# Order of work at the head of an FFN stage, and one ScalarE copy in a block product

## The chip, the cores and the metric

The kernel runs on one core of a Trainium2 chip. The metric is the time of one execution in microseconds on the device, as the median of several runs. Five engines work side by side, each through its own queue in program order: TensorE (matmuls, out of SBUF into PSUM), VectorE, ScalarE, GpSimd (POOL in the profile) and SyncE (SP, which issues most of the loads).

## The reference

A trunk of two layers over 512 tokens of width 1024, in fp32. Each layer is a gated FFN, a token mixer and a second gated FFN; each of the three takes a normalised input that is scaled and shifted by a vector from the condition c (adaLN).

```python
c_act = jax.nn.silu(c)
for l in range(DEPTH):                      # DEPTH = 2
    mod = c_act @ ada_w[l] + ada_b[l]       # nine vectors of 1024
    ...
    f = swiglu(modulate(rmsnorm(h, ln_ffn1[l]), sh1, sc1), ffn1_wg[l], ffn1_wu[l], ffn1_wd[l])
    h = h + MACARON_WEIGHT * gt1[:, None, :] * f
    ...                                     # the mixer, then the second FFN in the same form
# swiglu(x, wg, wu, wd) = (silu(x @ wg) * (x @ wu)) @ wd, inner width 2816
```

## The kernel before

**Layout and precision.** The activations are held transposed, 128 features by 512 tokens a tile. Each fp32 matmul is done as three faster ones: both operands are split into a rounded high half and a low half (`wh`, `wl` for a weight, `uh`, `ul` for the normalised input, `ah`, `al` for the FFN's inner columns), and high by high, high by low and low by high are added up in PSUM. ScalarE makes a high half with a copy, VectorE the low half with a subtraction (`halves`, L300; `split`, L888).

**Stages.** The program is FFN, mixer, FFN, for two layers: four FFN stages, which begin near 0, 1060, 1430 and 2425 us, and two mixers. The weights come as units of 128 output columns, in a fixed list. `w_split` (L317) splits the next unit or part of a unit; `w_ahead(lead)` (L353) goes on splitting until `lead` quarters of a unit lie ready; `w_get` (L357) takes a unit and then splits ahead by `4 * ahead` quarters, 7 in an FFN stage. `w_fill` (L349) keeps 3 or 4 units of raw weights ordered from SP.

**FFN inner columns.** There are 22 of them, each with a gate and an up product. The first four (six in the first stage) are plain products: `dense`, 24 matmuls of 512 tokens. Of these the first two columns (four in the first stage) are multiplied already at the end of the stage before, in `tail` (L629) or `start` (L782), and handed on as PSUM banks `pss`. The other columns go in pairs through `dense_pair` (L389): a 2 by 2 block product in seven parts instead of eight, each 12 matmuls of 256 tokens, in three banks mX, mZ and mY. The parts use sums and differences of blocks of the weights (`ws`, made by POOL and by accumulating loads) and of the input (`th`, `tl`, made by `halves_sums`, L590: half by POOL, half by VectorE). The parts go X, Z, X, Y, X, Z, X; after each, ScalarE copies the bank into `c`, or VectorE adds the bank to `c`, and a part that accumulates further in the same bank has to wait for that. Down products follow after two or three pairs, in four chunks.

**What sets the order.** Each engine works through its instructions in the order in which the program emits them. Work that runs beside the products lies in lanes of generators (`run`, `step`, L174): every third (in a pair every sixth) matmul makes a `tick`, and at a tick each generator in the lane `post` goes one step, if an estimated clock that the program keeps says that its inputs are there. The sums of the input, the gates and the products of a pair run in that lane; `drain("post")` before the first pair (L935) and before each down chunk (L946) emits what is left of it. At each tick `ada_tick` (L470) also adds `rate` to a counter, and at 1 a step of adaLN is emitted: one load of 256 KB four steps ahead, and one VectorE operation with c. What is not done by the first down chunk is done there at one go (`ada_need`, L478).

**Head of a stage.** At the end of `tail`, after the halves of the input are made, `w_ahead(4)` (L775; 12 ahead of the mixer) splits one unit, `halves_sums` is put in the lane, and the last products of the first columns are emitted. Then `ffn` (L895) loads c anew and computes its silu (`c_load`, L156; `c_silu`, L162: a tanh on ScalarE and one VectorE operation for each half of c), and finishes the first columns one after the other: tanh on ScalarE, `g` and `ay` on VectorE, `ah` on ScalarE, `al` on VectorE. Nearly all tiles come from one pool of 84 buffers (`NBIG`); a load or an operation that takes a buffer waits until its last reader is done.

Of the kernel before, what the change touches and what calls it, by code (L numbers as in the profile page):

```python
# [58 lines left out]
def trunk(ctx: ExitStack, tc: tile.TileContext, x, c, ada_w, ada_b, ln, w_gu, w_dn, w_in, w_ba, conv_w,  # L59
# [17 lines left out]
    def big(s, shape=(128, 512), dt=F32):  # L77
        return bigp.tile(list(shape), dt, name=nm(s), tag="big")
# [77 lines left out]
    def c_load():  # L156
        for i in range(2):
            caT[i] = big("ca")
            nc.sync.dma_start(out=caT[i], in_=bass.AP(tensor=c.tensor, offset=c.offset + 512 * i,
                                                      ap=[[0, 128], [1, 512]]))  # L160

    def c_silu():  # L162

        for i in range(2):
            t = big("ct")
            A.activation(out=t, in_=caT[i], func=AF.Tanh, scale=0.5)
            V.scalar_tensor_tensor(out=caT[i], in0=t, scalar=1.0, in1=caT[i], op0=OP.add, op1=OP.mult)
# [185 lines left out]
    def w_ahead(lead):  # L353
        while st["split"] < len(jobs) and st["lead"] < lead:
            w_split()
# [26 lines left out]
    def dense(key, xs):  # L382
        w = w_get(key)
        ps = bank("mm")
        lst = passes(w, xs, range(len(xs)))
        mm_list([(ps, a, b, i == 0, i == len(lst) - 1) for i, (a, b) in enumerate(lst)])
        return ps

    def dense_pair(keys, us, ts):  # L389

        X, Y, Z = bank("mX"), bank("mY"), bank("mZ")
        c1, c2 = big("c1"), big("c2")
        lo, hi = HALF

        def b(k0, sl):
            return [(us[k][0][:, sl], us[k][1][:, sl]) for k in range(k0, k0 + 4)]

        def copy(out, ps):  # L400
            A.activation(out=out, in_=ps[:, lo], func=AF.Copy)

        def add(out, ps):
            V.tensor_tensor(out=out, in0=ps[:, lo], in1=out, op=OP.add)

        for j, (ps, x, first, fn, out) in enumerate((
                (X, b(0, lo), True, copy, c1[:, lo]), (Z, ts[0], True, copy, c2[:, hi]),
                (X, ts[1], False, copy, c1[:, hi]), (Y, b(4, lo), True, add, c1[:, lo]),
                (X, ts[2], False, add, c2[:, hi]), (Z, b(4, hi), False, add, c1[:, hi]),
                (X, ts[3], False, copy, c2[:, lo]))):  # L410
            w = w_get(keys[0], part=j)
            lst = passes(w, x, range(4), lo)
            mm_list([(ps[:, lo], a_, b_, first and i == 0, i == len(lst) - 1)
                     for i, (a_, b_) in enumerate(lst)], 2 * Q)
            fn(out, ps)
        return c1, c2
# [212 lines left out]
    def tail(keys, xs, gt, nxt, Gs, adds):  # L629
# [142 lines left out]
            low = nlow  # L772
            mm_list(lt[8 + 3 * k:11 + 3 * k])
        low()
        w_ahead(12 if any(narrow) else 4)  # L775
        ts = None if any(narrow) else halves_sums(yt)
        for k in range(NF):
            first(k, 1)
# [3 lines left out]
    def start(l, keys):  # L782
# [99 lines left out]
        for g in (64, 96):  # L882
            V.tensor_tensor(out=sel, in0=sel, in1=ident[:, g:g + 16], op=OP.add)
        w_fill()
        w_ahead(4)
        return us, pss, halves_sums(ys)

    def split(y, s):  # L888
# [6 lines left out]
    def ffn(l, f, us, pss, ts, nxt):  # L895
        act = {}
        st.update(ahead=AHEAD, raw=4)
        ada.update(rate=0.13, stop=min(len(ada_seq), 144 * l + 96 * f + 80))
        if (l, f) != (0, 0):
            c_load()  # L900
            c_silu()
        seq = ffn_order(first_gu(l, f))

        def gate(cs, done):

            for c_, sign in zip(cs, (0.5, -0.5)):
                t = big("t")
                A.activation(out=t, in_=c_, func=AF.Tanh, scale=sign)
                yield
                V.scalar_tensor_tensor(out=c_, in0=t, scalar=1.0, in1=c_, op0=OP.add, op1=OP.mult)  # L910
                done.append(c_)
                yield

        def product(i, gs, done, ups):
            for j, (c_, y) in enumerate(zip(gs, ups)):
                while len(done) <= j:
                    yield False
                V.tensor_tensor(out=y, in0=c_, in1=y, op=OP.mult)
                yield
                act[i + j] = split(y, "a")  # L920
                yield
        gt = None
        for kind, i in seq:
            if kind == "gu":
                pg, pu = (pss.pop(0) if pss else dense(("gu", l, f, i, q), us) for q in range(2))
                t = big("t")
                A.activation(out=t, in_=pg, func=AF.Tanh, scale=0.5)
                g2 = big("g2")
                V.scalar_tensor_tensor(out=g2, in0=t, scalar=1.0, in1=pg, op0=OP.add, op1=OP.mult)
                y = big("ay")  # L930
                V.tensor_tensor(out=y, in0=g2, in1=pu, op=OP.mult)
                act[i] = split(y, "a")
            elif kind == "pair":
                if i == first_gu(l, f):
                    drain("post")  # L935
                g2s = dense_pair([("pair", l, f, j, 0) for j in (i, i + 1)], us, ts)
                done = []
                run("post", gate(g2s, done))
                ups = dense_pair([("pair", l, f, j, 1) for j in (i, i + 1)], us, ts)
                run("post", product(i, g2s, done, ups))  # L940
            else:
                if gt is None:
                    g_ = ada_need(l, 6 * f + 2)
                    gt = small("gt", [128, NF])
                    V.tensor_scalar(out=gt, in0=g_, scalar1=0.25, scalar2=None, op0=OP.mult)
                drain("post")  # L946
                lo, hi = CHUNKS[i]
                xs = [act.pop(j) for j in range(lo, hi)]
                last = i == len(CHUNKS) - 1
                st["ahead"] = 4 if last else AHEAD  # L950
                if last:
                    ada["rate"] = 0.0
                    Gs = gains(*nxt[:2]) if nxt else (None, None)
                    adds = []
                o = 0
                while o < (NF - TAIL if last else NF):
                    if last and o:
                        st["ahead"] = 3 + o
                    if last and o == 0:
                        pd = dense_late([("dn", l, f, i, q) for q in range(3)], xs)  # L960
                    else:
                        pd = [dense(("dn", l, f, i, o), xs)]
                    for p in pd:
                        V.scalar_tensor_tensor(out=h[o], in0=p, scalar=gt[:, o:o + 1], in1=h[o],
                                               op0=OP.mult, op1=OP.add)
                        if last:
                            norm_acc(o, adds)
                        o += 1
        return tail([("dn", l, f, i, q) for q in range(NF - TAIL, NF)], xs, gt, nxt, Gs, adds)


# [632 lines left out]
```

## Time and profile before

| | us |
|---|---|
| median of three runs | 2786.26 |
| the three runs | 2776.88, 2786.26, 2789.63 |
| the profiled execution | 2783.32 |
| its span, from the first to the last instruction | 2781.5 |

| engine | busy us | share of the span |
|---|---|---|
| TensorE | 2687.2 | 97% |
| VectorE | 2014.8 | 72% |
| ScalarE | 1262.1 | 45% |
| GpSimd | 867.1 | 31% |

The times of rows are counted from the first instruction. PE is TensorE, DVE VectorE, ACT ScalarE, POOL GpSimd. A row names the tile that is written, an arrow and the tiles that are read. What stands in square brackets or behind the last bar is the idle time of the engine before it, and which instruction ended it.

### The profile page before, as it was taken

Reading aid. Unit: us, or ns where it says so; the run is one execution under the profiler, and the core shown is the slowest. Engines: PE = TensorE matmul, PEld = TensorE weight load, DVE = VectorE, ACT = ScalarE, POOL = GpSimd, SP = SyncE. Lnnn points to the kernel's source line nnn. Section 1 sums busy time; section 2 is a strip of 40 time slices with the busy share of each in tenths; the row PEclk is TensorE's granted clock in tenths of the full one; section 3 lists DMA queues with packets and bytes.
Section 4 is the critical chain, followed back from the end, with each engine's and each line's share of the span. In section 5 each row is a group of like instructions: output and inputs, shape, how many; then the busy total and the mean of one; then the engine's idle time right before and its main releaser. Section 6 shows DMA issues by size and latency. Waiting matters only on the chain.

```text
span 2781.5 us, 48295 instructions
## 1 busy us (share of the span) xinstructions
PE 2687.2 (97%) x17332; PEld 2372.4 (85%) x17332; DVE 2014.8 (72%) x3889; ACT 1262.1 (45%) x2594; POOL 867.1 (31%) x1285
## 2 busy tenths in 40 slices
PE   6899999999999998999989999999999999989998
PEld 4789998888878888899988989888888888989997
DVE  8787878676655678787788877776665566787676
ACT  5344445555533334454444544445554333354443
POOL 4232304453450005123142322254445200224231
PEclk9999999999999999999999999999999999999999
DMA  7476732342344545766536776323323546256552
GB/s 275 132 221 183 180 109 95 107 120 74 109 137 152 172 143 153 206 189 179 166 102 196 192 189 164 130 68 111 103 75 101 152 163 220 90 167 175 144 147 65
DMA packets 254529, 407.12 MB, mean 146 GB/s; under 512 B 52816, under 2 KB 69968, under 8 KB 254288
## 3 DMA queue, kind: packets, MB, share of 16 engines
q1 hardware_dynamic: 231568, 358.93, 40.6%
q0 software_dynamic: 22720, 45.10, 9.2%
q8 instruction: 136, 2.23, 0.3%
q14 instruction: 105, 0.86, 0.1%
HBM read 382.95 MB, written 11.53 MB: 142 GB/s over the span
## 4 chain that ended last, share of the span: by engine, by line
PE 85%; DVE 8%; ACT 2%; issue 2%; DMA 2%; POOL 0%; SPq 0%; DVEq 0%; ACTq 0%
PE mm L122 50%; PE mX L122 13%; PE mZ L122 6%; PE tl L122 4%; PE mY L122 3%; DVE wl L122 3%; PE as L122 1%; DVE c L122 1%; PE ob L122 1%; DVE ad L122 1%; PE pw L122 1%; PE pq L122 1%; PE aT L122 1%; PE po L122 1%; DVE tl L122 1%
## 5 line engine op out<-in xcount | busy, mean ns | idle before, releaser
L122 DVE TENSOR_TENSOR wl<-wr,wh 128x512 fp32r<-128x512 f32 (+1 forms) x936 | 676.7, 757 | 180.0 <-ACT wh L122 175.1
L122 ACT ACTIVATE wh<-wr 128x512 fp32r<-128x512 f32 (+1 forms) x936 | 517.1, 595 | 143.7 <-PE mm L122 110.8
L122 PE MATMUL mm<-uh,wh 128*128 128x512 f32 (+1 forms) x1488 | 411.9, 385 | 36.7 <-ACT wh L122 24.7
L122 PE MATMUL mm<-uh,wl 128*128 128x512 f32 (+1 forms) x1488 | 406.7, 378 | 0.0
L122 PE MATMUL mm<-ul,wh 128*128 128x512 f32 (+1 forms) x1488 | 357.1, 374 | 1.6 <-DVE ul L122 1.6
L122 PEld LDWEIGHTS mm<-uh,wh 128*128 128x128 f32 x1488 | 276.7, 193 | 87.5 <-ACT wh L122 27.2
L122 PEld LDWEIGHTS mm<-uh,wl 128*128 128x128 f32 x1488 | 278.9, 191 | 44.4 <-issue 0.7
L122 PEld LDWEIGHTS mm<-ul,wh 128*128 128x128 f32 x1488 | 256.6, 189 | 44.3 <-DVE ul L122 2.3
L122 ACT ACTIVATE c<-mX 128x256 f32<-128x256 f32 x210 | 80.5, 383 | 367.0 <-PE mX L122 366.4
L293 POOL DMA_DIRECT2D wr<-in_w_gu_dram x70 | 61.6, 880 | 512.3 <-DVE wl L122 189.4
L122 DVE SCALAR_TENSOR_TENSOR ad<-ad,ca 128x512 f32<-128x512 f32 x272 | 193.6, 726 | 0.4 <-PE mm L122 0.2
L122 POOL TENSOR_SCALAR y<-y,G,mod 128x256 f32<-128x256 f32 (+1 forms) x88 | 64.7, 737 | 350.5 <-DVE y L122 200.8
L122 POOL TENSOR_TENSOR ws<-wr,wr 128x512 f32<-128x512 f32 x70 | 97.4, 1392 | 225.2 <-DMA wr<-in_w_gu_dram 40.5
L122 DVE TENSOR_TENSOR wl<-ws,wh 128x512 fp32r<-128x512 f32 x210 | 161.4, 775 | 7.8 <-ACT wh L122 6.1
L122 PE MATMUL mm<-ah,wh 128*128 128x512 f32 x608 | 159.7, 391 | 1.3 <-ACT wh L122 1.0
L122 PE MATMUL mm<-ah,wl 128*128 128x512 f32 x608 | 158.2, 389 | 0.0
L122 PE MATMUL mX<-th,wh 128*128 128x256 f32 x840 | 138.7, 288 | 20.0 <-DVE c L122 17.8
L122 PE MATMUL mm<-al,wh 128*128 128x512 f32 x608 | 158.0, 389 | 0.0
L122 DVE SCALAR_TENSOR_TENSOR h<-mm,gt,h 128x512 f32<-128x512 f32 x120 | 88.9, 748 | 80.9 <-PE mm L122 80.6
L122 PEld LDWEIGHTS mX<-th,wh 128*128 128x128 f32 x840 | 115.9, 192 | 25.2 <-DVE c L122 21.6
L122 PE MATMUL mX<-tl,wh 128*128 128x256 f32 x840 | 135.8, 284 | 0.0
L122 PE MATMUL mX<-th,wl 128*128 128x256 f32 x840 | 135.6, 284 | 0.0
(318 smaller groups left out, 5400.5 us busy)
## 6 DMA issues: line engine op xcount, KB each, us to landing
wr<-in_w_gu_dram SPq DMA_DIRECT2D x352, 256.0 KB, 4.3
ad<-in_ada_w_dram SPq DMA_DIRECT2D x288, 256.0 KB, 4.2
wr<-in_w_in_dram SPq DMA_DIRECT2D x264, 256.0 KB, 3.2
wr<-in_w_dn_dram SPq DMA_DIRECT2D x128, 256.0 KB, 3.2
ws<-in_w_gu_dram SPq DMA_DIRECT2D x70, 256.0 KB, 4.3
wr<-in_w_gu_dram POOLq DMA_DIRECT2D x70, 256.0 KB, 4.3
ws<-in_w_gu_dram POOLq DMA_DIRECT2D x70, 256.0 KB, 6.5
wr<-in_w_dn_dram SPq DMA_DIRECT2D x96, 128.0 KB, 3.1
```

The lines of the kernel that those rows point to most:

```text
L122: return fn(*args, **kw)
L293: nc.gpsimd.dma_start(out=out, in_=src, accum_op=OP.add)
```

## The change

The change has four parts. (1) In `tail` and in `start`, `w_ahead(12)` splits three units at the head of each stage instead of one (ahead of the mixer it was 12 already). (2) In `ffn` the columns that are handed on as banks are finished stage by stage: all tanh, then all `g` and `ay`, then all splits. (3) In the three later FFN stages c is still loaded at once, but its silu is computed by a generator after 24 ticks, and adaLN steps start only then. (4) In the fifth of the seven parts of `dense_pair`, ScalarE copies the bank mX to a new tile `c3`, and VectorE adds `c3` to `c` instead of adding the bank.

```diff
         c1, c2 = big("c1"), big("c2")
+        c3 = big("c3")[:, :256]
...
+        def copy_add(out, ps):
+            copy(c3, ps)
+            V.tensor_tensor(out=out, in0=c3, in1=out, op=OP.add)
...
-                (X, ts[2], False, add, c2[:, hi]), (Z, b(4, hi), False, add, c1[:, hi]),
+                (X, ts[2], False, copy_add, c2[:, hi]), (Z, b(4, hi), False, add, c1[:, hi]),
...
-        w_ahead(12 if any(narrow) else 4)
+        w_ahead(12)
...
         w_fill()
-        w_ahead(4)
+        w_ahead(12)
         return us, pss, halves_sums(ys)
...
         if (l, f) != (0, 0):
+            ada["rate"] = 0.0
             c_load()
-            c_silu()
+
+            def late():
+                for _ in range(24):
+                    yield False
+                c_silu()
+                ada["rate"] = 0.13
+
+            run("post", late())
...
         gt = None
-        for kind, i in seq:
+        there = [(pss[2 * i], pss[2 * i + 1]) for i in range(len(pss) // 2)]
+        tanhs, ys = [big("t") for _ in there], [big("ay") for _ in there]
+        for (pg, _), t in zip(there, tanhs):
+            A.activation(out=t, in_=pg, func=AF.Tanh, scale=0.5)
+        for (pg, pu), t, y in zip(there, tanhs, ys):
+            V.scalar_tensor_tensor(out=t, in0=t, scalar=1.0, in1=pg, op0=OP.add, op1=OP.mult)
+            V.tensor_tensor(out=y, in0=t, in1=pu, op=OP.mult)
+        for i, y in enumerate(ys):
+            act[i] = split(y, "a")
+        for kind, i in seq[len(there):]:
             if kind == "gu":
-                pg, pu = (pss.pop(0) if pss else dense(("gu", l, f, i, q), us) for q in range(2))
+                pg, pu = (dense(("gu", l, f, i, q), us) for q in range(2))
```

## Rows read from the trace of the kernel before

**Rows 1.** The page's first part: busy time, share of the span, instructions.

```profile
PE 2687.2 (97%) x17332; PEld 2372.4 (85%) x17332; DVE 2014.8 (72%) x3889; ACT 1262.1 (45%) x2594; POOL 867.1 (31%) x1285
```

**Rows 2.** TensorE's waits: who for whom; us in total, times, longest.

```profile
PE mm L122 <- ACT wh L122: 25.8, 6, 6.7
PE mX L122 <- DVE c L122: 17.8, 19, 2.2
...
PE mZ L122 <- ACT th L122: 7.9, 1, 7.9
...
PE mX L122 <- ACT c L122: 2.2, 3, 1.0
```

**Rows 3.** Busy time by stretch: length, each engine (instructions), granted clock, DMA share, GB/s.

```profile
90.60:95.12 4.52, 4.52 (x11) 3.55 (x12) 4.45 (x11) 3.55 (x7) 1.57 (x2) 0.50 0.64 104
118.97:122.43 3.46, 3.46 (x16) 3.46 (x17) 2.70 (x5) 2.68 (x6) 0.00 (x0) 0.50 0.15 24
193.80:197.50 3.70, 3.70 (x19) 3.70 (x19) 1.55 (x4) 0.90 (x2) 1.78 (x2) 0.54 0.44 86
1070.10:1076.79 6.69, 0.00 (x2) 0.00 (x1) 5.01 (x8) 2.49 (x6) 0.00 (x0) 0.85 0.62 196
1076.79:1081.57 4.78, 4.78 (x11) 3.84 (x12) 4.78 (x6) 4.07 (x8) 4.24 (x4) 0.50 0.15 55
...
2442.30:2446.90 4.60, 4.60 (x11) 3.63 (x12) 4.60 (x6) 4.07 (x8) 4.05 (x4) 0.50 0.16 57
...
1099.00:1139.00 40.00, 38.33 (x314) 37.88 (x315) 32.85 (x63) 20.63 (x46) 5.89 (x5) 1.00 0.64 189
```

**Rows 4.** Timeline of TensorE, head of the second FFN stage: start, us, instructions.

```profile
1068.13 1.98 PE L122 MATMUL mm<-ul,wh 128*128 128x512 f32 x8
1076.79 3.78 PE L122 MATMUL mm<-uh,wh 128*128 128x512 f32 x8 [6.69 <-ACT wh L122]
```

**Rows 5.** Timeline of ScalarE, the same head.

```profile
1072.81 0.63 ACT L122 ACTIVATE ah<-ay 128x512 fp32r<-128x512 f32 x1 [2.54 <-DVE ay L122]
...
1076.12 2.17 ACT L122 ACTIVATE wh<-wr 128x512 fp32r<-128x512 f32 x4
```

**Rows 6.** Timeline of VectorE, the same head.

```profile
1057.66 1.29 DVE L122 TENSOR_TENSOR wl<-wr,wh 128x512 fp32r<-128x512 f32 x2
...
1070.02 1.28 DVE L122 SCALAR_TENSOR_TENSOR ca<-ct,ca 128x512 f32<-128x512 f32 x2
...
1073.47 0.69 DVE L122 TENSOR_TENSOR al<-ay,ah 128x512 fp32r<-128x512 f32 x1 [0.78 <-ACT ah L122]
...
1076.86 4.11 DVE L122 TENSOR_TENSOR wl<-wr,wh 128x512 fp32r<-128x512 f32 x4
```

**Rows 7.** Timelines of TensorE and VectorE, head of the first FFN stage.

```profile
90.60 3.78 PE L122 MATMUL mm<-uh,wh 128*128 128x512 f32 x8 [4.70 <-ACT wh L122]
...
79.42 0.69 DVE L122 SCALAR_TENSOR_TENSOR g<-t,mm 128x512 f32<-128x512 f32 x1 [8.47 <-ACT t L122]
...
90.67 2.49 DVE L122 TENSOR_TENSOR wl<-wr,wh 128x512 fp32r<-128x512 f32 x4
```

**Rows 8.** Timelines of VectorE and ScalarE in a later pair of columns.

```profile
1285.88 1.77 DVE L122 SCALAR_TENSOR_TENSOR c<-t,c 128x512 f32<-128x512 f32 x1
...
1290.71 0.38 ACT L122 ACTIVATE c<-mX 128x256 f32<-128x256 f32 x1 [5.12 <-PE mX L122]
```

**Rows 9.** Groups of instructions: count, busy us, mean ns, idle before, what ended it.

```profile
L122 ACT ACTIVATE wh<-wr 128x512 fp32r<-128x512 f32 (+1 forms) x936 | 517.1, 595 | 143.7 <-PE mm L122 110.8 <-DVE wl L122 26.0 <-DMA wr<-in_w_gu_dram 3.7
...
L122 DVE SCALAR_TENSOR_TENSOR ad<-ad,ca 128x512 f32<-128x512 f32 x272 | 193.6, 726 | 0.4 <-PE mm L122 0.2
...
L122 ACT ACTIVATE c<-mX 128x256 f32<-128x256 f32 x210 | 80.5, 383 | 367.0 <-PE mX L122 366.4
...
L122 DVE TENSOR_TENSOR c<-mX,c 128x256 f32<-128x256 f32 x70 | 29.4, 420 | 4.2 <-PE mX L122 3.6
```

**Rows 10.** The page's part on loads: count, KB each, median us to landing.

```profile
ad<-in_ada_w_dram SPq DMA_DIRECT2D x288, 256.0 KB, 4.2
```

## The prediction

> **What bounds the kernel now.** I read the share of each engine first: TensorE is busy for 97% of the span [rows 1], so a change can only win what TensorE waits, and what it loses in clock after a wait. The second view is TensorE's waits by releaser [rows 2]: 25.8 us in six waits for a rounded weight (wh) from ScalarE, 17.8 us in nineteen waits of a product's bank mX for VectorE's add into c, 7.9 us in one wait for a rounded sum (th). The third view is the granted clock by stretch [rows 3]. In the 6.69 us without a matmul at 1070 the clock falls, and the next 4.78 us run at 0.50, the lower level of 1.2 GHz, so half of them, 2.4 us, is lost on top. At 193.80, after one of the longest waits on mX (2.2 us [rows 2]), it is near 0.5 for 3.4 of 3.7 us: 1.7 us lost.
>
> So there are three sums to win. **Heads of the three later FFN stages** (1070, 1439, 2436 us): the 25.8 us less 4.7 us in the first stage [rows 7] and about 1 us elsewhere leave 20 us; with half of 4.8, 4.3 (taken between its neighbours) and 4.6 us at the lower clock [rows 3], 27 us. **First stage**: 4.7 us [rows 7] and 7.9 us [rows 2], with half of 4.52 and of 3.46 us [rows 3]: 16.5 us. **Bank mX**: 17.8 us [rows 2] and twice 1.7 us [rows 3] (a second such stretch follows one more of the longest waits): 21 us. Together 64 us of an execution of 2783.3 us.
>
> Why TensorE waits at a head: ScalarE rounds the four halves that it needs at 1076.12 [rows 5], in program order behind the two splits ah, and those wait for VectorE's ay. VectorE is in one unbroken queue from the last low half of u on: two wl for the one unit that is split early (1057.66), the sums until 1070.02, c's silu (2 in 1.28 us), then the two finished columns with a stop of 0.78 us before an al, since ah of the same column is only then on its way [rows 6]. The weights stand behind all of it.
>
> **Part 1, three units split ahead (tail and start).** The units for the next dense products are split before the sums are queued. This moves four wh (0.54 us each, from 2.17 us for four [rows 5]) and four wl forward. Alone, four wl take 2.49 us [rows 7]; beside POOL (busy for 4.24 of the 4.78 us there [rows 3]) 4.11 us [rows 6]. They now stand right behind the two wl that went at their plain 1.29 us [rows 6], so I take 2.5 us; the upper bound is 4.1. They delay the sums by that, and TensorE needs no sum until the first pair. TensorE's program is unchanged: 8 matmuls of 512 columns take about 1.8 us [rows 4], less their overlap, a unit 5.5. Its second, third and fourth unit now go 1070.1, 1075.6, 1081.0, and the first pair begins at 1086.5; now it is 1076.79 and three units and the 2.4 us of slow clock, 1095.7: 9 us later. The fourth unit is split after the two finished columns; VectorE's queue to there is six wl (3.7 us), the sums (11 us from 1058.9 to 1070.0 [rows 6]) and two columns without stops (4.2): about 1077, and two wl more make 1078, for need at 1081 to 1083. The loads are no issue: the raw weights are ordered earlier, and ScalarE's wh waited for a weight load for 3.7 us in the whole run [rows 9].
>
> **Part 2, first columns stage by stage.** Both tanh go first, then both g and y, then the splits. The adds and multiplies are the same; the stops of 0.78 us before al [rows 6] go, 1.5 us of VectorE at a later head and 3 us in the first stage, where there are four columns. Banks come free no later. Cost nothing, since ScalarE is idle there (2.54 us before one ah [rows 5]).
>
> **Part 3, c later.** The silu of c (1.28 us of VectorE at 1070.02 [rows 6]) moves behind 24 ticks, three dense products. With it the first adaLN step moves from the first to the fourth unit, and its four loads are only ordered then. Two prices. A load takes 4.2 us to land [rows 10], behind up to five other loads on SP's queue; VectorE reaches the step at about 1088 (1078, a column 2.9, seven wl 4.4, the last low sums 1.2, c's silu 1.3), and behind it in its queue stand the product of the fourth unit and the weights of the pair's second half, needed at 1096.6. A late landing costs TensorE between 0 and about 4 us a head; I take 0.5, since seven parts (10 us of TensorE) are split by then. Second, three steps fewer are done by the first down product, where the rest is done in one go: 3 times 0.73 us [rows 9] more in VectorE's queue, 2.2 us, of which 0 to 2.2 reach TensorE; no wait of its own stood there before, so I take 0.3.
>
> A later head then gives 9 less 0.5, less 0.5 for the tighter queue at the pair, so 8; three give 24 us, a last subtraction for the down product leaves 23. **First stage:** VectorE idles 8.47 us before the first g [rows 7]; the four wl move into that hole and save 2.5 us, the stops 3 us. TensorE's 4.7 us disappear, but it then stands longer for th, which is released by VectorE's whole queue: the gain is the queue's, 5.5 to 6.5 us, not 16. I take 6; the bounds are 3 (POOL's second sum sets the end) and 10.
>
> **Part 4, the closest half product copied by ScalarE.** Of the seven parts, the fifth and the seventh both use mX, with only the sixth (12 matmuls of half the width, about 1.4 us) between. VectorE's add of the fifth is 0.42 us [rows 9], but stands in its queue behind operations that POOL stretches: at 1285.88 one of 1.77 us [rows 8], with a wait of TensorE behind it. ScalarE then stands idle for 5.12 us, until its next copy at 1290.71 [rows 8]. A copy of this shape takes 0.38 us there [rows 9], 70 of them 27 us off the path. What ScalarE's copies out of mX already cost shows in the same view: 2.2 us in three waits, out of 140 such hand-overs [rows 2]; one more in 70 pairs costs about 1.1 us. So 21 less 1: 20 us. The lower bound is 0, if VectorE's lateness stops TensorE at the weights instead; VectorE is busy 32.85 of 40 us with two pairs [rows 3], and the seven parts of lead are 10 us against a lateness of 2, so I take 20.
>
> Against this stands a rule. The add had one operand in PSUM and keeps at 420 ns in the mean over 70 [rows 9]; its new form reads two SBUF operands, as wl does, whose four took 2.49 us in one place and 4.11 us beside POOL's adds [rows 6, 7]. The Trainium skill (SBUF — State Buffer, "Who interferes with whom") says that VectorE and GpSimd share one pair of SBUF ports under a lock, and that a VectorE operation with two SBUF inputs falls under it. The trace agrees. By that rule each add could wait for a GpSimd operation. By rows alone the price is at most 1.77 less 0.6 us [rows 8], 1.2 us of VectorE in a pair of 20 us, and it is off TensorE's path so long as VectorE has its 18% of slack; it is counted in the second rival.
>
> **Sum.** 23 + 6 + 20 = 49 us off the profiled execution of 2783.3 us: 2734. That execution lies 3 us below the median of the runs shown, so 2737 us. With all of 27, 10 and 21 it would be about 2728; with the weak ends of the parts (15, 3, 13) 2755: own range 2724 to 2757, with the spread of runs.
>
> **Rivals.** *The head's wait only changes its releaser* (to th, or to the parts of the first pair). For it: the first stage, where 7.9 us stand for th right after the weights were there, behind a VectorE queue that is as full at the later heads. Against: there the second sums are queued early, ahead of the finished columns. The heads would give 5 instead of 23: 2755. Chance 0.14.
>
> *VectorE is the bound in the pairs.* Waits on mX go, and come back as waits for wl. For it: 82% busy with POOL's stretches, and the port lock. Against: its lateness of 2 us against a lead of 10. mX gives 2 instead of 20: 2755. Chance 0.13.
>
> *Buffers, slower.* The later products, tanh tiles and four more split tiles hold some 8 of the pool's 84 buffers longer, and c3 one in each pair; loads on SP wait for buffers. If loads go late enough, wh waits for data. Each of 70 pairs would pay what its load is late beyond its lead; it decides when a weight lands more than about 10 us later than now. At 1.5 us a pair it is 105 us, less the 49: 2843. Against: the 3.7 us of such waits [rows 9], which say that loads have room. Chance 0.06.
>
> *The reordering does little*: the order in which the sums are queued follows an estimated clock, which the earlier splits shift, so that gains at the heads and mX are mostly given back in the same stage. About 2776. Chance 0.09.
>
> **How the numbers follow.** Forecast 0.58 at 2737. The first two rivals are faster too. A difference under 0.5% (14 us) is about what cannot be told from none here. Faster: 0.58 + 0.14 + 0.13 = 0.85, less 0.01 for their tails: 0.84; same 0.09; slower 0.07. The range goes from 2722, all parts full and a fast median, to 2765, which takes in both faster rivals; it leaves out the last two.
>
> **What would show it.** Right: no wait of several us for wh at the later heads and no lower clock there; mX waits for ScalarE in a few waits of under 1 us; at the first stage one wait, for th, longer than 7.9 us but ending some 6 us earlier. Wrong: mZ or mX at the first pair of a head waiting for th or wl, a VectorE stop before the first adaLN step released by its load, or mm waiting at the first down product. The forecast falls if such new waits add up to over 20 us.

## The result and the profile after

| | before | after |
|---|---|---|
| median, us | 2785.11 (4 runs, 2776.88 to 2789.63) | 2742.46 (4 runs, 2740.16 to 2743.25) |
| ratio, 95% interval | | 0.9849 [0.9825, 0.9873] |
| profiled execution | 2783.32 | 2742.23 |
| its span | 2781.5 | 2740.4 |

The change saves 43 us, 1.5%. The page of the kernel after begins with the span and the busy times:

```profile
span 2740.4 us, 48441 instructions
...
PE 2677.2 (98%) x17332; PEld 2369.2 (86%) x17332; DVE 2005.9 (73%) x3889; ACT 1286.4 (47%) x2664; POOL 867.1 (32%) x1285
```

TensorE does the same 17332 matmuls. Its busy time is 10.0 us shorter than in [rows 1], with a mean granted clock of 0.993 instead of 0.990; the other 31.1 of the 41.1 us of span are idle time of TensorE that is gone. Which waits went is told by its waits (who for whom; us in total, times, longest):

```profile
PE mX L122 <- ACT c L122: 14.0, 5, 5.2
...
PE mZ L122 <- ACT th L122: 5.5, 2, 4.6
...
PE mm L122 <- ACT wh L122: 1.6, 4, 0.8
```

Against [rows 2], the 17.8 us for VectorE's add into c are gone altogether, 25.8 us for a weight have become 1.6, and 7.9 us for th have become 5.5. One line is new in size: mX for ScalarE's copy into c, 2.2 us before, is now 14.0 us. Three of its five waits, 12.8 us, stand at the three later heads, and the clock falls behind each. Three stretches by window, each from such a wait's end on (length, then busy time of PE, PEld, DVE, ACT, POOL with instructions, granted clock, DMA share, GB/s):

```profile
1080.23:1084.30 4.07, 4.07 (x19) 4.07 (x20) 2.72 (x7) 2.36 (x6) 0.00 (x0) 0.50 0.65 209
...
1436.70:1442.70 6.00, 6.00 (x28) 6.00 (x29) 4.06 (x9) 2.68 (x6) 0.00 (x0) 0.50 0.67 218
...
2424.18:2429.20 5.02, 5.02 (x23) 5.02 (x24) 4.58 (x7) 2.68 (x6) 1.53 (x1) 0.50 0.54 160
```

So the lower clock of [rows 3] is not gone from the heads; it has moved a few microseconds on.

Since both kernels issue their matmuls in one and the same order, the n-th matmul can be looked up in both timelines, and the difference of its two starts tells what has been won up to there. Read at the borders of the stages:

| part of the execution | won, us | forecast, us |
|---|---|---|
| start and head of the first stage | 0.1 + 8.2 | 6 |
| heads of the second, third and fourth stage | 2.9 + 3.6 + 3.6 = 10.1 | 23 |
| pairs and what follows, four stages | 6.7 + 8.3 + 5.5 + 3.3 = 23.8 | 20 |
| first mixer | -0.8 | 0 |
| sum | 41.4 | 49 |

The heads gave less than half of what was forecast. Here is the second head, on TensorE, ScalarE and VectorE (timelines: start, us, instruction; in brackets the idle time before and what ended it):

```profile
1072.04 0.64 PE L122 MATMUL mX<-uh,wh 128*128 128x256 f32 x4
...
1074.43 0.64 PE L122 MATMUL mZ<-tl,wh 128*128 128x256 f32 x4
1080.23 1.22 PE L122 MATMUL mX<-th,wh 128*128 128x256 f32 x4 [5.16 <-ACT c L122]
```

```profile
1075.12 0.57 ACT L122 ACTIVATE t<-mm 128x512 f32<-128x512 f32 x1
1078.76 0.63 ACT L122 ACTIVATE ah<-ay 128x512 fp32r<-128x512 f32 x1 [3.07 <-DVE ay L122]
1079.30 0.61 ACT L122 ACTIVATE wh<-wr 128x512 fp32r<-128x512 f32 x1
1079.82 0.36 ACT L122 ACTIVATE c<-mX 128x256 f32<-128x256 f32 x1
```

```profile
1071.17 1.29 DVE L122 TENSOR_TENSOR wl<-wr,wh 128x512 fp32r<-128x512 f32 x2
...
1075.38 1.28 DVE L122 SCALAR_TENSOR_TENSOR ca<-ct,ca 128x512 f32<-128x512 f32 x2
1076.59 0.68 DVE L122 SCALAR_TENSOR_TENSOR ad<-ad,ca 128x512 f32<-128x512 f32 x1
...
1077.98 0.69 DVE L122 TENSOR_TENSOR ay<-g,mm 128x512 f32<-128x512 f32 x1
```

The pair begins at 1072.04. Its first part fills bank mX by about 1073.6, and its third part goes into the same bank. ScalarE's copy that empties the bank stands in ScalarE's queue behind ah of the fourth column, the last one ahead of the pairs. That ah waits for VectorE's ay, and ay is the end of a VectorE queue without a gap from 1070.56 on: a low half al, the low halves of the pair's first weights, c's silu, an adaLN step, g, ay. ScalarE idles for 3.07 us with the copy behind it, and TensorE for 5.16.

The same chain was there before. These are the same steps in the kernel before, on TensorE and on ScalarE:

```profile
1095.47 0.64 PE L122 MATMUL mX<-uh,wh 128*128 128x256 f32 x4
...
1099.15 0.75 PE L122 MATMUL mX<-th,wh 128*128 128x256 f32 x4 [0.65 <-ACT c L122]
```

```profile
1097.68 0.63 ACT L122 ACTIVATE ah<-ay 128x512 fp32r<-128x512 f32 x1 [5.02 <-DVE ay L122]
1098.21 0.61 ACT L122 ACTIVATE wh<-wr 128x512 fp32r<-128x512 f32 x1
1098.73 0.36 ACT L122 ACTIVATE c<-mX 128x256 f32<-128x256 f32 x1
```

The copy was already late, by 0.65 us. All three waits of the line mX for ScalarE in [rows 2] stand at this place of the three later heads: 0.65, 1.03 and 0.57 us. The whole program stands 14.2 us earlier at this head. From 1095.47 to 1072.04 are 23.4 us, so the pair begins 9.2 us earlier on top of that; ah goes from 1097.68 to 1078.76, 18.9 us, only 4.7 on top. And 0.65 + 9.2 - 4.7 = 5.2 us, the wait that is measured. TensorE was moved ahead by 9, VectorE's queue by 4.7, and a head can win no more than the queue does; of these 4.7 the lower clock takes half of 4.07 us back.

### The profile page after: what moved, and what is told of

The parts are those of the page before. It is cut to its first block, busy times and chain, and to the rows that moved or that the text cites. A ratio compares the mean times of both kernels' runs of the same rounds, so it can differ in the third digit from the quotient of the medians.

```text
span 2740.4 us, 48441 instructions
## 1 busy us (share of the span) xinstructions
PE 2677.2 (98%) x17332; PEld 2369.2 (86%) x17332; DVE 2005.9 (73%) x3889; ACT 1286.4 (47%) x2664; POOL 867.1 (32%) x1285
## 3 DMA queue, kind: packets, MB, share of 16 engines
q1 hardware_dynamic: 231568, 358.93, 41.1%
## 4 chain that ended last, share of the span: by engine, by line
PE 90%; DVE 4%; DMA 2%; ACT 2%; issue 1%; SPq 0%; POOL 0%; DVEq 0%; ACTq 0%
PE mm L122 53%; PE mX L122 13%; PE mZ L122 6%; PE tl L122 4%; PE mY L122 4%; PE as L122 1%; PE ob L122 1%; DVE ad L122 1%; PE pw L122 1%; PE pq L122 1%; PE aT L122 1%; PE po L122 1%; DVE wl L122 1%; DMA wr<-in_w_gu_dram 1%; ACT wh L122 1%
## 5 line engine op out<-in xcount | busy, mean ns | idle before, releaser
L122 DVE TENSOR_TENSOR wl<-wr,wh 128x512 fp32r<-128x512 f32 (+1 forms) x936 | 666.9, 747 | 157.3 <-ACT wh L122 154.9
L122 PE MATMUL mm<-uh,wh 128*128 128x512 f32 (+1 forms) x1488 | 404.7, 379 | 11.8 <-ACT uh L122 11.8
L122 ACT ACTIVATE c<-mX 128x256 f32<-128x256 f32 x280 | 107.2, 383 | 320.6 <-PE mX L122 319.0
L122 PEld LDWEIGHTS mm<-ah,wh 128*128 128x128 f32 x608 | 112.8, 188 | 27.6 <-ACT wh L122 3.3
```

The source lines that it names most:

```text
L122: return fn(*args, **kw)
```

## The experiments

**Theory**: what the heads lack is this order on ScalarE, the copy behind ah; take the fourth column's split out of the way and the rest comes. **First rival**: VectorE is simply full there, and the wait would turn to a weight or a sum. **Second rival**: the parts of the change are worth something else than their terms, part 1 (the three units) above all. All medians are of four runs, each beside the kernel before on the same chip; the kernel after was run in a round of its own. The kernel before had medians of 2785.11 beside the kernel after, 2785.67 and 2785.78 in the next two rounds, and 2782.70 in the round of the last two kernels of the table, so a difference of some 3 us between two rounds is not a sure one.

| kernel | median, us | ratio, 95% interval |
|---|---|---|
| part 4 alone | 2760.66 | 0.9905 [0.9883, 0.9926] |
| without part 4 | 2760.60 | 0.9905 [0.9881, 0.9928] |
| without part 1 | 2744.20 | 0.9845 [0.9819, 0.9871] |
| without part 2 | 2748.27 | 0.9869 [0.9853, 0.9886] |
| without part 3 | 2754.13 | 0.9893 [0.9878, 0.9908] |
| fourth column's split later | 2726.07 | 0.9781 [0.9760, 0.9802] |
| c later still | 2735.96 | 0.9824 [0.9807, 0.9841] |
| first stage: VectorE's sums at once | 2739.53 | 0.9838 [0.9823, 0.9852] |
| split later, and one sum early | 2719.70 | 0.9765 [0.9741, 0.9789] |
| the same, and c later still | 2719.28 | 0.9765 [0.9740, 0.9789] |

**Part 4 alone.** The kernel before with ScalarE's copy:

```diff
-                (X, ts[2], False, add, c2[:, hi]), ...
+                (X, ts[2], False, copy_add, c2[:, hi]), ...
```

> The kernel before with the ScalarE copy in the fifth part (part 4) and nothing else. Theory, the terms stand by themselves: the waits of mX for VectorE's add go, 17.8 us in nineteen, with the lower clock behind the longest; some 21 us less than before (ratio 0.992 to 0.993), and the three waits of 6.7 us for wh at the later heads stay. Rival, VectorE is the bound in the pairs: its lateness comes back as waits for wl or at the next bank, and 5 us or less are won (ratio above 0.998).

It saves 25 us. TensorE's waits:

```profile
PE mm L122 <- ACT wh L122: 25.5, 5, 6.7
...
PE mZ L122 <- ACT th L122: 7.8, 1, 7.8
PE mX L122 <- ACT c L122: 4.7, 4, 1.7
```

The heads keep their waits for wh and th. All 17.8 us for VectorE are gone, and 2.5 us more for ScalarE have come, so the rival of the prediction that VectorE is the bound in the pairs falls: no wait for wl took their place.

**Without part 4.** The kernel after with VectorE's add instead of the copy:

```diff
-                (X, ts[2], False, copy_add, c2[:, hi]), ...
+                (X, ts[2], False, add, c2[:, hi]), ...
```

> The changed kernel without the copy (parts 1 to 3 alone). Theory, the terms stand by themselves: 20 us less than before (ratio 0.993), of which the first stage gives 8 and the three later heads 11 together; mX waits for VectorE's add again, about 18 us in all. Rival, the head needs the copy: with TensorE earlier at the first pair VectorE's add is later against it, mX waits grow by 2 us or more a head, and less than 14 us are won (ratio above 0.995).

Parts 1 to 3 alone save 25 us too. With part 4 that would be 50, and the whole change saves 43. TensorE's waits show some of the overlap:

```profile
PE mX L122 <- DVE c L122: 13.4, 15, 2.0
PE mX L122 <- ACT c L122: 12.7, 3, 5.0
```

The earlier parts had already taken 4.4 of the 17.8 us that part 4 takes. The long waits for ScalarE at the three heads are there without part 4's copy as well, so that copy does not make them.

**Fourth column's split later.** The kernel after, with ah and al of the fourth column emitted at the eighth tick of the first pair instead of ahead of it:

```diff
-                act[i] = split(y, "a")
+                if i == first_gu(l, f) - 1:
+                    fourth = (i, y)
+                else:
+                    act[i] = split(y, "a")
...
                     drain("post")
+                    def finish(i_, y_):
+                        for _ in range(7):
+                            yield False
+                        act[i_] = split(y_, "a")
+                    run("post", finish(*fourth))
```

> The changed kernel, with the split (ah, al) of the last single column emitted at the eighth tick of the first pair instead of ahead of the pair. Theory, ScalarE's queue: the first copy out of mX stands behind this ah, which waits for VectorE's ay; with ah out of the way the waits of 5.2, 3.8 and 3.9 us at the first pairs of the later heads shrink to about 1.5 us each and the lower clock behind them goes: 12 to 16 us less than the changed kernel (2727 to 2730 us). Rival, VectorE is the bound at the head: the copy is early, but TensorE then waits for wl or for VectorE's adds a few parts later; 4 us or less are won.

It saves another 16.4 us against the kernel after, without any work less. ScalarE's timeline at the second head, then TensorE's busy time and clock from 1072 on:

```profile
1072.51 0.58 ACT L122 ACTIVATE t<-mm 128x512 f32<-128x512 f32 x1
1072.98 0.62 ACT L122 ACTIVATE wh<-wr 128x512 fp32r<-128x512 f32 x1
1073.50 0.37 ACT L122 ACTIVATE c<-mX 128x256 f32<-128x256 f32 x1
...
1077.27 0.64 ACT L122 ACTIVATE ah<-ay 128x512 fp32r<-128x512 f32 x1 [0.22 <-DVE ay L122]
```

```profile
1072.00:1112.00 40.00, 38.49 (x321) 38.29 (x320) 36.99 (x68) 24.30 (x54) 9.44 (x8) 1.00 0.71 200
```

The copy now starts at 1073.50, 0.3 us after the bank is full, three copies of the pair pass ahead of ah, and the clock stays at full speed. The waits at the first block product are gone altogether, not shrunk to 1.5 us each as expected. What is left is a wait of 1.51 us at the second block product of the same columns (at 1086.25), where the copy stands behind the tanh of a gate, which waits for VectorE's add into c; the other two heads keep 0.79 and 1.12 us there. By the starts of the same matmuls the three heads now give 10.1, 10.3 and 9.9 us against the kernel before, of which the second block product takes 1.8, 1.0 and 1.4 us back. The theory holds, and the first rival falls: VectorE, busy for 37 of those 40 us, delivers in time.

**Without part 1.** The kernel after with one unit split ahead:

```diff
-        w_ahead(12)
+        w_ahead(12 if any(narrow) else 4)
...
-        w_ahead(12)
+        w_ahead(4)
```

> The changed kernel with one unit split ahead at the head of an FFN stage, as before (part 1 undone). Theory, part 1 carries the heads: TensorE waits for wh again at the three later heads (5 to 6 us each, since the columns' order and the later c save VectorE 2 to 3 us) with the lower clock behind, and in the first stage; the waits for ScalarE's copy at the first pair are gone; 8 to 16 us more than the changed kernel (2750 to 2758 us). Rival, the order of the columns and the later c are enough: 3 us more or less.

It costs 1.7 us, too little to be told from none. TensorE's waits, and the one at the second head in its timeline:

```profile
PE mm L122 <- ACT wh L122: 13.3, 9, 4.0
...
PE mZ L122 <- ACT th L122: 9.3, 2, 6.3
...
PE mX L122 <- ACT c L122: 1.7, 3, 0.7
```

```profile
1062.65 3.56 PE L122 MATMUL mm<-uh,wh 128*128 128x512 f32 x8 [3.96 <-ACT wh L122]
```

The waits for a weight are back (3.96, 3.16 and 3.97 us at the heads), and the waits for the copy are gone. TensorE waits either in front of the dense products or behind them; the queue that it waits for is the same. So at the later heads of this kernel part 1 only moves a wait: by the starts of the same matmuls they give 12.6 us without it. (A trace can differ by as much as these 2.5 us: the kernel with VectorE's sums at once, below, has the later heads of the kernel after and gives 12.6 there too.) What part 1 wins lies in the first stage, whose head gives 4.6 us without it instead of 8.2. The second rival holds for part 1. Whether part 1 is worth more once the fourth column's split is out of the way was not run.

**Without part 3.** c's silu and the adaLN steps at once, as before:

```diff
-            ada["rate"] = 0.0
             c_load()
...
-            run("post", late())
+            c_silu()
```

> The changed kernel with c's silu at once and the adaLN steps from the first tick, as before (part 3 undone). Theory, VectorE's queue: ahead of the last single column's ay now stand c's silu and four steps instead of c's silu and one, 1.8 us more a head, so the waits at the first pairs grow by that: 5 to 7 us more than the changed kernel (2748 us). Rival, part 3 brings nothing of its own and only loads later: the same within 1 us, or up to 2 us less.

It costs 11.7 us, twice what was expected. TensorE's wait at the second head, and VectorE ahead of the ay on which it hangs:

```profile
1086.32 1.23 PE L122 MATMUL mX<-th,wh 128*128 128x256 f32 x4 [8.36 <-ACT c L122]
```

```profile
1070.03 1.77 DVE L122 SCALAR_TENSOR_TENSOR ad<-ad,ca 128x512 f32<-128x512 f32 x1
...
1078.80 2.35 DVE L122 TENSOR_TENSOR wl<-ws,wh 128x512 fp32r<-128x512 f32 x2
1081.07 1.74 DVE L122 TENSOR_TENSOR wl<-wr,wh 128x512 fp32r<-128x512 f32 x1
...
1084.13 0.69 DVE L122 TENSOR_TENSOR ay<-g,mm 128x512 f32<-128x512 f32 x1
```

The waits at the heads are 8.36, 4.93 and 8.37 us here, 3.2, 1.1 and 4.5 more than in the kernel after, where 1.8 each was expected. The longer queue counts as such, and at this head more of it is stretched besides: operations that take 0.69 us elsewhere take 1.74 to 1.77. By the starts of the same matmuls the three heads give nothing without part 3 (-1.0, 3.3 and -2.4 us). So part 3 is the largest part of what parts 1 to 3 win, and what the heads won is its work.

**Without part 2.** One loop for each column, as before:

```diff
-        for (pg, _), t in zip(there, tanhs):
+        for i, ((pg, pu), t, y) in enumerate(zip(there, tanhs, ys)):
             A.activation(out=t, in_=pg, func=AF.Tanh, scale=0.5)
-        for (pg, pu), t, y in zip(there, tanhs, ys):
             ...
-        for i, y in enumerate(ys):
             act[i] = split(y, "a")
```

> The changed kernel with the columns that are handed on finished one after the other, as before (part 2 undone). Theory: VectorE stops 0.7 to 0.8 us before each al again, 1.5 us at a later head and 3 us in the first stage, all of it in the queue that releases TensorE: 6 to 9 us more than the changed kernel (2750 us). Rival, VectorE's stops are hidden because other work in its queue waits anyway: 2 us more or less.

It costs 5.8 us. Most of it is in the first stage, with its four columns; TensorE there:

```profile
110.23 1.10 PE L122 MATMUL mZ<-th,wh 128*128 128x256 f32 x2 [7.39 <-ACT th L122]
115.17 0.58 PE L122 MATMUL mZ<-th,wh 128*128 128x256 f32 x1 [3.84 <-ACT th L122]
```

In the kernel after, the same two waits are 0.93 and 4.57 us, 5.7 us less.

By the starts of the same matmuls against the kernel before, one trace each, us:

| kernel | head of the first stage | three later heads |
|---|---|---|
| the kernel after | 8.2 | 10.1 |
| without part 1 | 4.6 | 12.6 |
| without part 2 | 2.0 | 11.0 |
| without part 3 | 7.5 | -0.1 |

Parts 1 and 2 work in the first stage, part 3 at the later heads.

**c later still.** c's silu behind forty ticks instead of twenty-four, in a lane of its own that is emptied only at the first down product:

```diff
-                for _ in range(24):
+                for _ in range(40):
...
-            run("post", late())
+            run("c", late())
...
                 if gt is None:
+                    drain("c")
```

> The changed kernel with c's silu and the adaLN steps moved on to the 40th tick, inside the first pair. Theory, one VectorE queue up to the last single column's ay releases ScalarE's copy: c's silu (1.3 us) and one adaLN step (0.6 us) stand ahead of that ay, so the three waits at the first pairs shrink by 1.8 us each: 5 to 7 us less than the changed kernel (2736 us). Rival, the wait is set by something else (ScalarE's own work, the bank): no difference beyond 1 us, or 1 to 3 us more, since two more steps fall to the first down product.

It saves 6.5 us against the kernel after by the medians, but its four runs lie from 2731.23 to 2739.39, and the trace is of the slowest, 2.8 us under that of the kernel after. The waits at the heads fall to 3.23, 2.17 and 1.98 us, by 1.9, 1.6 and 1.9, as an ay with c's silu no longer ahead of it should make them. The price shows at the first down product, in TensorE's timeline:

```profile
1129.01 1.66 PE L122 MATMUL mm<-ah,wh 128*128 128x512 f32 x6 [1.50 <-ACT wh L122]
```

That wait (1.50, 1.50 and 1.46 us in the three later stages) is the burst of adaLN steps that the prediction priced at 0.3 for the kernel after; there it is 0.22 to 0.28 us.

**First stage, VectorE's sums at once.** The kernel after, with VectorE's half of the input's sums emitted ahead of the finished columns:

```diff
         for k0 in range(2):
-            run("post", make(k0))
+            if k0 in now:
+                for _ in make(k0):
+                    pass
+            else:
+                run("post", make(k0))
...
-        return us, pss, halves_sums(ys)
+        return us, pss, halves_sums(ys, now=(1,))
```

> The changed kernel with VectorE's half of the input sums emitted at once in the first stage, ahead of its first columns, in the hole in which VectorE waits for the first tanh. Theory, the first stage's wait for th (0.9 and 4.6 us, with 2.5 us of clock) is VectorE's queue: it goes but for 1 to 2 us, 6 to 8 us less than the changed kernel (2735 us). Rival, POOL's half or ScalarE's queue sets the end: 2 us less, or more, if the first columns are late.

It saves 2.9 us by the medians, under half of what was expected, and the traces don't show it won in the first stage. TensorE's two waits there, and VectorE:

```profile
84.84 3.59 PE L122 MATMUL mm<-uh,wh 128*128 128x512 f32 x8 [4.89 <-DVE t L122]
...
110.90 0.51 PE L122 MATMUL mZ<-th,wh 128*128 128x256 f32 x2 [0.81 <-ACT th L122]
```

```profile
73.80 1.40 DVE L122 TENSOR_TENSOR ta<-y,ta 128x256 f32<-128x256 f32 x1
75.23 1.40 DVE L122 TENSOR_TENSOR tb<-ta,y 128x256 f32<-128x256 f32 x1
...
84.10 0.68 DVE L122 SCALAR_TENSOR_TENSOR t<-t,mm 128x512 f32<-128x512 f32 x1
```

The wait for th is nearly gone, so it was VectorE's queue that set its end. But both sums, some of their operations stretched to 1.40 us, do not fit into VectorE's hole: the first g (written over the tile t) starts at 84.10 instead of 79.22, a bank comes free 5 us late, and TensorE waits for that. One wait stands for the other: up to the end of the first stage both kernels have won 15 us against the kernel before. What the trace has over that of the kernel after lies at the later heads (12.6 us instead of 10.1), which the edit does not touch.

**Both together.** The split later, and only the first of VectorE's two sums early:

```diff
-        for k0 in range(2):
-            run("post", make(k0))
+        gens = [make(k0) for k0 in range(2)]
+        for _ in range(now):
+            next(gens[1])
+        for g_ in gens:
+            run("post", g_)
...
-        return us, pss, halves_sums(ys)
+        return us, pss, halves_sums(ys, now=4)
```

> The kernel with the later split of the fourth column, and in the first stage only the first of VectorE's two sums (four steps, about 3 to 4 us of VectorE) emitted ahead of the first columns, in the hole in front of the first tanh. Theory: the hole holds one sum but not two, so TensorE is not kept from its banks (under 1 us, against 4.9 us with both sums), and th comes 3 us earlier: 3 to 5 us less than with the later split alone (2722 us). Rival: POOL beside it stretches the sum past the hole, and what th wins is lost at the banks: within 1 us (2726 us).

2719.70 us: 22.8 us under the kernel after and 2.35% under the kernel before, so a version that beats both. It lies 6.4 us under the split later by the medians, which are of two rounds, and 2.8 us by the profiled executions; 3 to 5 us were expected. In the first stage TensorE waits 1.01 us for th and 1.75 us for a tl, instead of 0.93 and 4.57.

**And c later still, once more.** The same with c's silu behind 34 ticks in its own lane, and adaLN steps at a rate of 0.16 after it:

```diff
-                for _ in range(24):
+                for _ in range(34):
...
-                ada["rate"] = 0.13
-            run("post", late())
+                ada["rate"] = 0.16
+            run("c", late())
```

> The same with c's silu and the adaLN steps from the 34th tick, at a rate of 0.16 instead of 0.13. Theory: c's tanh (1.0 us of ScalarE) no longer stands ahead of the first copy out of mX, so the waits of 1.5, 0.8 and 1.1 us at the first pairs go: 2 to 3 us less (2720 us). Rival: ten ticks less of adaLN steps fall to the first down product, where 1 to 1.5 us of wait for ah or wh a stage come back, as with the 40th tick: no difference or 1 to 2 us more.

2719.28 us, no difference that can be told. The waits at the heads go from 1.22, 1.23 and 1.22 to 0.70, 1.09 and 0.76 us, 1.1 us in all. The theory had them in the wrong place: they stand at the second block product, behind the tanh of a gate, and not behind c's tanh at the first. The rival's price does not show either: the waits at the first down product are 0.22 to 0.29 us. With the split out of the way, moving c this far on wins nothing that can be told.

## Why the prediction came out as it did

The forecast was 2737 us, and 2742 was measured, inside the range. The sign and the three places were right; the split of the sum was not, and one term was mis-sized by half. That the time still came close is in part luck: the heads gave 13 us less than their term, the pairs and the first stage 6 us more. Of the signs of being right, no wait for wh at the later heads came true; no lower clock there, waits of mX under 1 us and a single wait for th did not. The sign of being wrong that came was mX at the first pair, for a copy where th or wl was named.

**Part 1 and the step that failed.** The pair's start was put at 1086.5, which is 1072.3 with the 14.2 us already won; it began at 1072.04. The fourth unit's split was put at 1078, so 1063.8; its low halves went at 1063.18. The weights, then, came as told. What failed is "less 0.5 for the tighter queue at the pair": it measured 5.16, 3.81 and 3.88 us, and 4 to 6 us of lower clock behind each. The prediction looked at VectorE's queue and the weights of the pair, and said that ScalarE is idle there. It was idle, but in order: the copy, whose bank was full at 1073.6, went at 1079.82, behind an ah that waited for ay until 1078.76. The Trainium skill (Perfetto Trace Analysis, "Tensor Engine Instruction (MATMUL, LD_WEIGHTS)") says that only TensorE's queue reorders anything, weight loads ahead of matmuls, and that the other compute engines execute strictly in order; the trace agrees, with 3.07 us of idle ScalarE in front of ah while the bank behind it stood full. The rival "the head's wait only changes its releaser" named this outcome, with th or the parts of the first pair as the new releaser, at a chance of 0.14, and gave the heads 5 us. They gave 10, between it and the forecast. The row that showed it was misread: the 2.2 us of [rows 2] were spread over 140 copies as a price, while all three waits stand at the first pairs of these heads. The argument for the first stage, that the gain is the queue's, held for all four heads and should have been applied to all. At the later heads the 9 us of part 1 are thus not its gain; what they won is part 3's.

**Part 2.** 1.5 us a later head and 3 in the first stage were forecast, 7.5 in all; without it the kernel is 5.8 us slower. The size was right, the place was not: without part 2 the waits at the later heads grow by 0.9 us in all (5.11, 4.72 and 3.95), those for th in the first stage by 5.7.

**Part 3.** It was counted as a cost of under 1 us a head and credited with no gain. Its costs came as told: VectorE waits for adaLN loads for 0.8 us in the whole run, and the burst costs 0.22 to 0.28 us at the first down product of a later stage. But it was worth 11.7 us, the most of the three, and all that the later heads won, since it takes operations out of the queue on which the heads hang. That was overlooked by the same mistake.

**First stage.** 6 us forecast, 8 won. The weights' 4.7 us went and th took their place, as forecast, and it is VectorE's queue that sets its end: the runs that move VectorE's sums ahead shorten it. But the last wait for th ends 9.0 us earlier (118.97 in [rows 3], 109.96 after), not 6, so in place of one wait longer than 7.9 us there are two of 5.5 together. The term that was too small is part 2's there, 3 us forecast and 5.7 measured.

**Part 4.** 20 us forecast; 23.8 in the pairs of the kernel after, and alone 25 by the medians and 23.1 between the profiled executions. The 17.8 us of waits went, and so did the two stretches of lower clock, 1.7 us each by the starts of the same matmuls. What the sum left out is a term beside each wait: behind 15 of the other 17 the matmuls win another 0.25 us, some 4 us in all, which the profile counts as busy time. It is no lost clock: behind the wait of 1.03 us at 1116.28, for one, the granted clock in the kernel before is 1.00. The price of 1.1 us for the new copies came true by luck, since none of the 2.2 us that it was worked out from is a wait within the pairs. In the kernel after the waits for copies outside the heads are 0.59 and 0.55 us; with part 4 alone there is one, of 1.67 us, and the three at the heads grow from 2.2 to 3.0.

**The rule on ports.** VectorE's groups, by form, in the kernel after (busy, mean ns, idle before):

```profile
L122 DVE TENSOR_TENSOR c<-c,c 128x256 f32<-128x256 f32 x70 | 34.7, 495 | 17.0 <-ACT c L122 16.1
L122 DVE TENSOR_TENSOR c<-mY,c 128x256 f32<-128x256 f32 x70 | 29.3, 418 | 20.7 <-PE mY L122 20.7
```

The add that now reads two SBUF operands went from 420 ns [rows 9] to 495; the adds that still read a bank stay at 418. The Trainium skill (SBUF — State Buffer, "Who interferes with whom") gives the reason as a lock on shared ports, and the trace agrees: 65 of the 70 adds keep at 0.41 to 0.43 us, and five take 1.30 to 1.51. All five begin while one of POOL's adds of weights is running, 0.39 to 0.46 us after its start. Of the 65, two overlap one, but begin 0.07 and 0.11 us ahead of it, and the ten that overlap only POOL's DMA issues are not held up. Of the adds that read a bank, seven begin while one of POOL's adds runs, and all take 0.41 to 0.42 us. One of the five and what POOL did at the time, in two timelines:

```profile
1192.71 1.51 DVE L122 TENSOR_TENSOR c<-c,c 128x256 f32<-128x256 f32 x1
```

```profile
1192.32 1.62 POOL L122 TENSOR_TENSOR ws<-wr,ws 128x512 f32<-128x512 f32 x1
```

The bound of 1.2 us for one such add was right (1.51 less 0.42 is 1.1), and all 70 cost 5.3 us of VectorE, off TensorE's path.

**Rivals that fell.** VectorE is not the bound in the pairs (part 4 alone). Late buffers: ScalarE's waits for a weight load rose from 3.7 us [rows 9] to 9.8, in three waits, but TensorE's waits for wh come to 1.6 us in the whole run, so little of it reached the path. And the sums came in time at the three later heads: TensorE waits for no th there.

## What to carry to other kernels

When work is moved ahead to end a wait, follow the waiting engine to its next three or four instructions and ask of each who frees its bank or makes its input; then read that engine's program order backwards to what it waits for, since an idle engine's next instruction can still stand behind one that is not ready. A head that hangs on one engine's unbroken queue can win no more than what that queue loses, however early the other inputs are; so shorten the queue, or let the one early instruction out of it. A wait of 0.65 us at such a place is worth reading: it says that the chain is already there, and that what is won in front of it can turn into it. And before a wait's total is used as a price for something new, see where its waits stand.

## What the runs showed of the hardware

Of VectorE's 70 adds of 128x256 with both operands in SBUF, the five that began while one of POOL's adds of weights was running took 1.30 to 1.51 us, the rest 0.41 to 0.43; the two that began just ahead of POOL's were not held up, nor were seven adds that read a bank. Other operations are held up by less as well: of the 1034 low halves of weights (128x512) in the kernel after, 888 take under 0.75 us, 89 from there to 1.5, and 57 up to 1.82. All of these 146 begin while POOL is at work on an add or a multiply; of the 845 that begin ahead of one or meet none, all are among the 888. A longer queue at a head can cost more than its plain sum: without part 3 the waits grow by 3.2, 1.1 and 4.5 us, where 1.8 each was worked out.

Behind pauses of 5.16, 3.81 and 3.88 us TensorE ran at 0.50, its lower level of 1.2 GHz, for 4 to 6 us; behind the pause of 1.51 us at 1086.25 in the kernel with the split later the 4.05 us that follow have a granted clock of 1.00. That a short pause is always free doesn't follow, and its length alone doesn't decide: in the kernel before, two pauses of 1.76 us, at 1288.65 and 1656.82, are followed by 0.63 over 4.55 us and 1.00 over 3.18 us. In the first stage of the kernel with the split later and one sum early, behind pauses of 1.01 and 1.75 us close together, the next 4.01 us have 0.68. What else decides it was not settled here.
